# The state-space operators of an encoder layer: arithmetic in finer pieces, rotation tables staged in two smaller buffers, copies moved to ScalarE

## The chip, the cores and the metric

The kernel runs on one core of a Trainium2 chip. The metric is the device time of one launch in microseconds (us). "The profile" is one execution recorded by the hardware profiler; its times count from the first instruction (the span's start).

## What is computed

One layer of a bidirectional encoder, 512 tokens of width 1024, in float32:

```python
h = h + 0.5 * swiglu(rms_norm(h, ffn1_norm), ffn1_w_gate, ffn1_w_up, ffn1_w_down)
q, k, v, x_ssm, g_attn, g_ssm = split(rms_norm(h, mix_norm) @ w_in)
y_attn = block_gqa_attention(rope(q), rope(k), v) @ w_attn_branch
y_s5 = s5_scan(x_ssm, forward) + s5_scan(x_ssm, backward) + ssm_d * x_ssm
z = gelu(y_s5); z = z * sigmoid(z @ ssm_glu_w + ssm_glu_b)
h = h + (sigmoid(g_attn) * y_attn + sigmoid(g_ssm) * (z @ w_ssm_branch)) @ w_out
h = h + 0.5 * swiglu(rms_norm(h, ffn2_norm), ffn2_w_gate, ffn2_w_up, ffn2_w_down)
h = h + sigmoid(rms_norm(h, ple_norm) @ ple_w_gate) * (p @ ple_w_proj)
```

`s5_scan` is a linear recurrence with 64 complex states in each of 32 groups of 16 channels, in both directions: with `lam_bar = exp(lam * delta)` each state follows `s[t] = lam_bar * s[t-1] + b_bar u[t]`, and the output is the real part of `c s`.

## The kernel before

**Products.** Every float32 operand of a large product is split into a high and a low part (`split`, L539 to L541: a cast on ScalarE, a subtraction on VectorE), and three matmuls of 128x512 stand for one (`mm3`, L555 to L557). Weights come in chunks of 128 x 1024 (`wchunk`): one transfer on SP's queue (L550), one cast (`w_..h`), one subtraction (`w_..l`), with four buffers each for raw, high and low.

**The FFN** (`ffn`, f0 to f21) works in two halves. A half first makes 11 columns of gate and up (`pg`, `pu`, then L680 to L683 and a split into `ah`, `al`), then 8 output tiles `pd` that contract over those 11 columns.

**The operators of the scan.** The recurrence runs over 64 chunks of 8 tokens. The matrices for it depend on parameters alone; the generator `ssm_params` makes them beside the first FFN and spills them to DRAM, and `ssm_prefetch` brings them back for two groups at a time, in 16 blocks. Its steps: exponentials, sine and cosine, powers of `lam_bar` and their arranged copies `pa`, `pb` (L225 to L228); transposes, and their spreading into `a_d` and `b_d` by 32 transfers on POOL's queue (L249, L250); four times a table `T` of rotations for 8 groups (L269 to L271, doubling its length six times), from which ScalarE copies two `tst` tiles (L301 to L303) and VectorE adds the decay (L305, with zeros at the edges, L306, L307), each written to `d_tb` (L308); then 8 times the output matrices and the block-diagonal `bd` (L337, L340); then lags; then 8 times the input matrices, read back from `a_d` and `b_d` (L405, L406). `T` and `tst` have one buffer each.

**What sets the order.** After every piece of the FFN `side` is called with that piece's weight (`SIDE`: 5.5 for a column pair, 4.5 and 3 for an output tile of the first and second half) and writes out pieces of the generator until their weights, the numbers that it yields, have used up the credit:

```python
credit[0] += w
while credit[0] > 0:
    credit[0] -= next(gen, 1e9)
```

The framework's planner then orders each engine's instructions: an instruction may go as soon as the planner's own reckoning has its inputs and its buffer free, and what was written out earlier goes first. The order of an engine is fixed afterwards, so an instruction that really waits holds all those behind it. The same holds for SP's and POOL's queues.

Of the kernel before, what the change touches and what calls it, by code (L numbers as in the profile page):

```python
# [7 lines left out]
F32 = mybir.dt.float32  # L8
# [9 lines left out]
P = 128  # L18
SEQ = 512
G = 32  # L20
NS = 64
# [5 lines left out]
TW = 3 * GB * NC_ + 3 * GB * NC_  # L27


def split3(nc, pool, src, dst, tag, nm, rb=1):  # L30
    """src (fp32) as an exact sum of three bfloat16 parts dst[0..2], all of src's shape."""
    r = pool.tile([P] + list(src.shape[1:]), F32, tag=tag, bufs=rb, name=nm)
    nc.scalar.copy(dst[0], src)
    nc.vector.tensor_sub(r, src, dst[0])
    nc.scalar.copy(dst[1], r)
    nc.vector.tensor_sub(dst[2], r, dst[1])


def mm6(nc, o, a, b, start, stop):
    """a^T b from the parts of a and b."""  # L40
    pairs = ((0, 2), (0, 1), (0, 0), (1, 1), (1, 0), (2, 0))
    for n, (i, j) in enumerate(pairs):
        nc.tensor.matmul(o, a[i], b[j], start=start and n == 0, stop=stop and n == 5)  # L43


def ssm_params(tc, nc, pk_, px, dp, k):
    """Generator: chunked-scan operators from the SSM parameters, spilled to DRAM."""
# [61 lines left out]
    def expm1_parts(x, shape, nm, lo, hi):  # L109
        """n and e^r - 1 with x = n ln2 + r."""  # L110
        xc = sm(shape, nm + "xc")
        V.tensor_scalar(xc, x, lo, hi, ALU.max, ALU.min)
        n = sm(shape, nm + "n")
        V.tensor_scalar(n, xc, 1.4426950408889634, MAGIC, mul, add)
        V.tensor_scalar_add(n, n, -MAGIC)
        r = sm(shape, nm + "r")
        V.scalar_tensor_tensor(r, n, -0.693359375, xc, mul, add)
        V.scalar_tensor_tensor(r, n, 2.12194440e-4, r, mul, add)
        q = sm(shape, nm + "q")
        V.tensor_scalar_mul(q, r, 1.0 / 5040)  # L120
        for c in (1.0 / 720, 1.0 / 120, 1.0 / 24, 1.0 / 6, 0.5, 1.0):
            V.scalar_tensor_tensor(q, q, c, r, add, mul)
        return n, q
# [18 lines left out]
    # sin and cos of theta and of 8 theta  # L142
# [25 lines left out]
    # sin = 2 s c ; cos - 1 = -2 s^2  # L168
# [6 lines left out]
    # powers a^0 .. a^8, rows j  # L175
# [20 lines left out]
    # (lam_bar - 1) / lam  # L196
# [18 lines left out]
    # input matrix, also placed block-diagonally over the directions  # L215
# [4 lines left out]
    # powers as the operators use them: pa[r] = a^(7-r) | a^r, pb[l] = a^(l+1) | a^(8-l)  # L220
    pa, pb = sm([P, 2, G, L], "pa", pool=pk_), sm([P, 2, G, L], "pb", pool=pk_)
    for ri, src in ((0, pwr), (1, pwi)):
        sg = src.rearrange("p j g -> p g j")
        for r in range(L):
            V.tensor_copy(pa[:NS, ri, :, r], sg[:NS, :, 7 - r])  # L225
            V.tensor_copy(pa[NS:, ri, :, r], sg[NS:, :, r])
            V.tensor_copy(pb[:NS, ri, :, r], sg[:NS, :, r + 1])
            V.tensor_copy(pb[NS:, ri, :, r], sg[NS:, :, 8 - r])  # L228
    yield 9
    # chunk input operators, built with (l, channel) on the partitions  # L230
# [23 lines left out]
    # per-chunk decay and the unit rotations by 8 theta, padded with a zero at both ends  # L254
# [11 lines left out]
    def cmul2(orr, oi, a, br, bi, t):  # L266
        """As cmul, a with real and imaginary parts along its first free axis; t[i] = a b_i."""
        for i, b in ((0, br), (1, bi)):
            V.tensor_mul(t[:, i], a, b.unsqueeze(1).broadcast_to([P, 2] + list(b.shape[1:])))  # L269
        V.tensor_sub(orr, t[:, 0, 0], t[:, 1, 1])  # L270
        V.tensor_add(oi, t[:, 0, 1], t[:, 1, 0])  # L271

    GH = 8
    for gh in range(0, G, GH):
# [9 lines left out]
        while n < NC_:  # L284
            br = rkl[:, 0].unsqueeze(2).broadcast_to([P, GH, n])
            bi = rkl[:, 1].unsqueeze(2).broadcast_to([P, GH, n])
            cmul2(T[:, 0, :, 1 + n:1 + 2 * n], T[:, 1, :, 1 + n:1 + 2 * n], T[:, :, :, 1:1 + n], br, bi,
                  tb[:, :, :, :GH * n].rearrange("p a r (g n) -> p a r g n", g=GH))
            n *= 2
            if n < NC_:  # L290
                sq = pw.tile([P, 2, GH], F32, tag="sq", bufs=2, name=f"sq{gh}_{n}")
                ta = pw.tile([P, 2, 2, GH], F32, tag="sqt", name=f"sqt{gh}_{n}")
                cmul2(sq[:, 0], sq[:, 1], rkl, rkl[:, 0], rkl[:, 1], ta)
                rkl = sq
        for b in range(gh // GB, (gh + GH) // GB):
            st = pw.tile([P, TW], F32, tag="w3", name=f"tst{b}")
            g0 = b * GB - gh
            N = GB * NC_
            v = lambda i, w=1: st[:, i * N:(i + w) * N].rearrange("p (g c) -> p g c", c=NC_)
            for ri in range(2):  # L300
                nc.scalar.copy(v(ri), T[:, ri, g0:g0 + GB, 1:NC_ + 1])  # L301
                nc.scalar.copy(v(2 + ri)[:NS], T[:NS, ri, g0:g0 + GB, 0:NC_])
                nc.scalar.copy(v(2 + ri)[NS:], T[NS:, ri, g0:g0 + GB, 2:NC_ + 2])  # L303
                dv = v(4 + ri)
                V.tensor_copy(dv, e8[:, b * GB:(b + 1) * GB].unsqueeze(2).broadcast_to([P, GB, NC_]))  # L305
                V.memset(dv[:NS, :, 0], 0.0)  # L306
                V.memset(dv[NS:, :, NC_ - 1], 0.0)  # L307
            nc.sync.dma_start(d["tb"][b], st)  # L308
        yield 9
    es.close()  # L310
    pw = es.enter_context(tc.tile_pool(name="pw2", bufs=1, reuse_waits="tile"))
    # matrices, GB groups at a time: chunk output and the lags inside a chunk
    dcol = sm([P, G // 8], "dcol", pool=pk_)
    nc.gpsimd.dma_start(dcol, k["ssm_d"].rearrange("(m q) -> q m", q=P))
    kt = sm([P, 2, G, CH], "kt", pool=pk_)
    sh = [P, GB, L, CH]
    flat = lambda t: t.rearrange("p g l c -> p g (l c)")
    for b in range(NB):
# [17 lines left out]
        bd = pw.tile([P, 2, GB, 2, CH], F32, tag="bd", name=f"bd{b}")  # L336
        V.memset(bd, 0.0)  # L337
        for dr in range(2):
            ps = slice(dr * NS, (dr + 1) * NS)
            V.tensor_copy(bd[ps, :, :, dr], bb[ps, :, gs])  # L340
# [13 lines left out]
        yield 7.2  # L354
    # lag 0: both directions and D; then all lags to DRAM, lag l_out - l_in = e - 7 in column block e
# [68 lines left out]
def ssm_prefetch(nc, sp, k, j):  # L424
    """The operators of GM groups, back from DRAM."""
# [5 lines left out]
    nc.sync.dma_start(tb, d["tb"][b].rearrange("p (i n) -> p i n", i=6)[:, :, q * NC_:(q + GM) * NC_])  # L431
# [7 lines left out]
def ssm_block(nc, sp, px, pre, U, j):  # L439
    """GM groups: chunk inputs, scan over chunks, outputs in PSUM."""  # L440
# [19 lines left out]
    # states, rotated into the real axis; forward on the lower partitions, backward on the upper,  # L460
    # each written so that column n holds what enters chunk n
# [35 lines left out]
# gates before the SSM and beside it  # L497
NG1, NG2 = 8, 4
# weights of a piece of the SSM operators' arithmetic beside a piece of the FFN
# [4 lines left out]
def kernel(  # L504
# [38 lines left out]
    def wchunk(src, k, n):  # L543
        """src [(k 128), n] in DRAM -> hi, lo tiles [128, k, n]."""
# [23 lines left out]
    def rsqrt_newton(pool, ms, shape, nm, eng=V):  # L568
        """ms ** -0.5: a first guess from the bits of ms (within 4%), then Newton's steps."""
# [26 lines left out]
    class Stat:  # L596
        """Sum of squares over the features, collected tile by tile."""
# [118 lines left out]
    with tc.tile_pool(name="f1", bufs=1, reuse_waits="tile") as fp, tc.tile_pool(name="pw", bufs=1, reuse_waits="tile") as pw:  # L716
# [8 lines left out]
        def side(w):  # L725
            """Emit as much of the operators' arithmetic as fits beside a piece of the FFN."""
            credit[0] += w
            while credit[0] > 0:
                credit[0] -= next(gen, 1e9)
# [27 lines left out]
    def proj_T(c0, done):  # L757
        """In four pieces: done(u w_in[:, c0:c0 + 128] transposed)."""
# [8 lines left out]
    def run(*gens):  # L767
        """Emit pieces of the generators in turns."""
# [4 lines left out]
    def proj_tok(banks, c0, n, kn):  # L773
        """Tokens on partitions: banks[t][:, :n] = u @ w_in[:, c0:c0+n], kn contraction tiles a chunk."""
# [30 lines left out]
    with tc.tile_pool(name="qp", bufs=1, reuse_waits="tile") as qp:  # L805
# [28 lines left out]
        # channels of the SSM  # L834
# [13 lines left out]
        # q, k, v with tokens on partitions  # L848
# [23 lines left out]
        # transposed q: hi and lo parts of a head stacked on the contraction axis  # L872
# [19 lines left out]
    # the SSM runs beside the gates  # L892
# [6 lines left out]
    def scores(hd):  # L899
        """Exponentials of a head's scores, queries on partitions, and the reciprocals of their sums."""  # L900
# [44 lines left out]
    # attention: scores of a head beside the product with v of the one before  # L945
# [30 lines left out]
    # SSM gate and branch, cut into pieces that run beside the attention  # L976
# [15 lines left out]
    def half(ww, mc, x, done):  # L992
        """Two output tiles of a product with 512 contraction rows, in four pieces."""
# [140 lines left out]
def _consts():  # L1134
    """Identity, and the RoPE tables in the kernel's token order: shapes alone."""
# [37 lines left out]
```

## Time and profile before

| | us |
|---|---|
| median of 3 runs | 1213.11 |
| lowest and highest | 1210.88, 1213.55 |
| span of the profiled execution | 1211.5 |
| TensorE busy in it | 1142.5 |
| VectorE busy in it | 789.2 |
| ScalarE busy in it | 483.4 |

The profile gives the span of its execution, from the first to the last instruction, and no other time of it; beside it stand the runs' times. Engines are named PE (TensorE), DVE (VectorE), ACT (ScalarE), POOL (GpSimd) and SP (its queue issues most transfers). An engine that is idle before an instruction is shown with the length of that wait and with what ended it.

### The profile page before, as it was taken

The page shows a single profiled execution, that of the slowest core. Times are in us where ns is not written, and L with a number is a line of the kernel's source. Part 1 is how long each engine was busy: PE and PEld are TensorE (multiplying, and loading weights), DVE is VectorE, ACT ScalarE, POOL GpSimd, SP SyncE. Part 2 cuts the span into 40 slices and gives each one's busy share as a digit, 9 for nine tenths or more (in the row PEclk, how much of TensorE's full clock was granted, in tenths as well). Part 3 has the DMA queues.
Part 4 walks back from the last instruction along what each step waited for, and adds up shares of the span by engine and source line. Part 5 has one row for each costly group of instructions (what it writes and reads, how often), then busy time and mean ns, then how long its engine had stood idle before and what let it go on. Part 6 is the DMA issues. An engine that isn't in the chain of part 4 may idle for free.

```text
span 1211.5 us, 16350 instructions
## 1 busy us (share of the span) xinstructions
PE 1142.5 (94%) x6092; PEld 939.8 (78%) x6092; DVE 789.2 (65%) x1673; ACT 483.4 (40%) x834; POOL 48.7 (4%) x81
## 2 busy tenths in 40 slices
PE   4999689999999999997997999999999999999998
PEld 3787567888878877876876878888888888888886
DVE  3894588997758985998856857654443334444543
ACT  4433345453434544634365833433222223323332
POOL 4105100000000000000000000000000000000100
PEclk9999798999999999999998999999999999999999
DMA  9429746644596899787633134423223433323422
GB/s 188 129 76 271 235 138 209 196 154 139 118 263 216 273 300 174 217 252 239 207 80 95 44 79 139 122 88 104 85 71 96 133 104 88 94 72 96 142 68 52
DMA packets 258240, 177.02 MB, mean 146 GB/s; under 512 B 38672, under 2 KB 239568, under 8 KB 258160
## 3 DMA queue, kind: packets, MB, share of 16 engines
q1 hardware_dynamic: 253776, 163.70, 46.9%
q0 software_dynamic: 3920, 11.15, 3.5%
q10 hardware_dynamic: 464, 1.11, 0.5%
q8 instruction: 48, 0.79, 0.3%
q14 instruction: 32, 0.26, 0.1%
HBM read 148.89 MB, written 38.63 MB: 155 GB/s over the span
## 4 chain that ended last, share of the span: by engine, by line
PE 62%; DVE 16%; DMA 14%; issue 3%; ACT 3%; SPq 1%; POOL 0%; DVEq 0%; ACTq 0%; POOLq 0%
PE pg L555 6%; PE pg L556 6%; PE pg L557 6%; PE pd L555 5%; PE pd L557 5%; PE pd L556 5%; PE pu L555 5%; PE pu L557 5%; PE pu L556 5%; DMA d_tb<-tst 4%; DMA br<-d_b 3%; DMA w<-in_ffn_w_up_dram 2%; PE po L555 1%; PE pge L557 1%; PE po L556 1%
## 5 line engine op out<-in xcount | busy, mean ns | idle before, releaser
L682 DVE TENSOR_TENSOR t<-pu,rb 128x512 f32<-128x512 f32 x44 | 30.3, 688 | 79.0 <-PE pu L557 78.7
L680 DVE TENSOR_TENSOR t<-pg,rb 128x512 f32<-128x512 f32 x44 | 30.3, 688 | 53.4 <-PE pg L557 51.5
L540 ACT CAST ah<-t 128x512 fp32r<-128x512 f32 x44 | 27.4, 622 | 58.4 <-DVE t L683 58.3
L700 DVE SCALAR_TENSOR_TENSOR h<-pd,h 128x512 f32<-128x512 f32 x32 | 22.0, 687 | 28.7 <-PE pd L557 28.7
L681 ACT ACTIVATE t<-t 128x512 f32<-128x512 f32 x44 | 27.7, 631 | 18.2 <-DVE t L680 14.5
L541 DVE TENSOR_TENSOR al<-t,ah 128x512 fp32r<-128x512 f32 x44 | 30.2, 686 | 7.0 <-ACT ah L540 6.8
L565 ACT ACTIVATE xh<-h,gains 128x512 fp32r<-128x512 f32 x32 | 22.7, 721 | 24.6 <-DVE h L700 21.9
L683 DVE TENSOR_TENSOR t<-t,t 128x512 f32<-128x512 f32 x44 | 30.3, 688 | 2.3
L912 DVE TENSOR_REDUCE nb<-sc 128x1 f32<-128x512 f32 x32 | 21.5, 683 | 8.6 <-PE sc L911 8.3
L915 ACT ACTIVATE p<-sc,nb,rq 128x512 f32<-128x512 f32 x32 | 24.9, 782 | 4.0 <-DVE nb L913 3.8
L1078 POOL DMA_DIRECT2D pin<-in_p_dram x8 | 4.2, 532 | 546.6 <-PE pd L556 541.5
L301 ACT COPY tst<-T 128x256 f32<-128x256 f32 x16 | 6.5, 406 | 47.2 <-DVE T L270 21.6
L566 DVE SCALAR_TENSOR_TENSOR xl<-h,gains,xh 128x512 fp32r<-128x512 f32 x32 | 23.8, 744 | 0.6 <-ACT xh L565 0.3
L541 DVE TENSOR_TENSOR pl<-ppt,ph 128x512 fp32r<-128x512 f32 x32 | 21.6, 682 | 2.7 <-ACT ph L540 2.6
L305 DVE COPY tst<-e 128x256 f32<-128x256 f32 x16 | 4.0, 290 | 29.6 <-DMA d_tb<-tst 29.6
L955 PE MATMUL ppt<-ident,p 128*128 128x128 f32 x128 | 21.0, 277 | 1.1 <-ACT p L915 1.1
L642 PE MATMUL xT<-ident,xt 128*128 128x128 f32 x32 | 7.8, 424 | 14.5 <-DMA xt<-in_x_dram 14.5
L955 PEld LDWEIGHTS ppt<-ident,p 128*128 128x128 f32 x128 | 16.6, 143 | 5.7 <-ACT p L915 1.5
L540 ACT CAST ph<-ppt 128x512 fp32r<-128x512 f32 x32 | 18.4, 586 | 6.0 <-PE ppt L955 5.3
L910 PE MATMUL sc<-kh,qT 128*128 128x512 f32 x32 | 14.1, 439 | 7.0 <-ACT p L915 7.0
L43 PE MATMUL pv<-U,wv 128*128 128x64 bf16 x384 | 15.0, 199 | 4.9 <-DMA wv<-d_wv 2.8
L43 PEld LDWEIGHTS <-wv 128*128 128x128 bf16 x384 | 13.2, 101 | 7.8 <-issue 4.2
(1966 smaller groups left out, 3888.6 us busy)
## 6 DMA issues: line engine op xcount, KB each, us to landing
w<-in_ffn_w_gate_dram SPq DMA_DIRECT2D x44, 512.0 KB
w<-in_ffn_w_up_dram SPq DMA_DIRECT2D x44, 512.0 KB
w<-in_w_in_dram SPq DMA_DIRECT2D x26, 512.0 KB
w<-in_ffn_w_down_dram SPq DMA_DIRECT2D x32, 384.0 KB
w<-in_ffn_w_down_dram SPq DMA_DIRECT2D x32, 320.0 KB
d_tb<-tst SPq DMA_DIRECT2D x8, 768.0 KB
d_wo<-wo SPq DMA_DIRECT2D x8, 768.0 KB
d_wv<-wv SPq DMA_DIRECT2D x8, 768.0 KB
```

The source lines that it names most:

```text
L43: nc.tensor.matmul(o, a[i], b[j], start=start and n == 0, stop=stop and n == 5)
L540: S.copy(hi, src)
L541: V.tensor_sub(lo, src, hi.bitcast(F32))
L555: T.matmul(o, ah, bh, start=start, stop=False)
L556: T.matmul(o, ah, bl, start=False, stop=False)
L557: T.matmul(o, al, bh, start=False, stop=stop)
L680: V.tensor_mul(t1, gu[0], rb)
L681: S.activation(t1, t1, AF.Silu)
L682: V.tensor_mul(t2, gu[1], rb)
L683: V.tensor_mul(t1, t1, t2)
L915: S.activation(p_, sc, AF.Exp, bias=nb[:, t:t + 1], scale=rq[:, t, hd:hd + 1], accum_out=sm[:, t:t + 1])
L955: T.transpose(pt[:, t * P:(t + 1) * P], pr[t][:, kt * P:(kt + 1) * P], ident)
```

## The change

The powers' arranged copies and the copies into `bd` go from VectorE to ScalarE. The generator yields after each doubling of `T` and after each `tst`, and twice per output matrix, with other weights. `tst` has two buffers and holds the decay once instead of twice, so its width falls from 6 to 5 blocks of 256; `ssm_prefetch` reads the decay block twice, in a transfer of its own. Two tiles `bds` are cleared once and used in turn instead of a `bd` cleared 8 times. Comments are dropped.

```diff
-TW = 3 * GB * NC_ + 3 * GB * NC_
+TW = 5 * GB * NC_
...
         for r in range(L):
-            V.tensor_copy(pa[:NS, ri, :, r], sg[:NS, :, 7 - r])
-            V.tensor_copy(pa[NS:, ri, :, r], sg[NS:, :, r])
-            V.tensor_copy(pb[:NS, ri, :, r], sg[:NS, :, r + 1])
-            V.tensor_copy(pb[NS:, ri, :, r], sg[NS:, :, 8 - r])
-    yield 9
+            nc.scalar.copy(pa[:NS, ri, :, r], sg[:NS, :, 7 - r])
+            nc.scalar.copy(pa[NS:, ri, :, r], sg[NS:, :, r])
+            nc.scalar.copy(pb[:NS, ri, :, r], sg[:NS, :, r + 1])
+            nc.scalar.copy(pb[NS:, ri, :, r], sg[NS:, :, 8 - r])
+    yield 5
...
                 rkl = sq
+            yield 1.0 + n / 20
         for b in range(gh // GB, (gh + GH) // GB):
-            st = pw.tile([P, TW], F32, tag="w3", name=f"tst{b}")
+            st = pw.tile([P, TW], F32, tag="w3", bufs=2, name=f"tst{b}")
...
-                dv = v(4 + ri)
-                V.tensor_copy(dv, e8[:, b * GB:(b + 1) * GB].unsqueeze(2).broadcast_to([P, GB, NC_]))
-                V.memset(dv[:NS, :, 0], 0.0)
-                V.memset(dv[NS:, :, NC_ - 1], 0.0)
+            dv = v(4)
+            V.tensor_copy(dv, e8[:, b * GB:(b + 1) * GB].unsqueeze(2).broadcast_to([P, GB, NC_]))
+            V.memset(dv[:NS, :, 0], 0.0)
+            V.memset(dv[NS:, :, NC_ - 1], 0.0)
             nc.sync.dma_start(d["tb"][b], st)
-        yield 9
+            yield 0.5
...
+    bds = [pw.tile([P, 2, GB, 2, CH], F32, name=f"bd{i}") for i in range(2)]
+    for bd in bds:
+        V.memset(bd, 0.0)
...
-        bd = pw.tile([P, 2, GB, 2, CH], F32, tag="bd", name=f"bd{b}")
-        V.memset(bd, 0.0)
+        yield 4.8
+        bd = bds[b % 2]
         for dr in range(2):
             ps = slice(dr * NS, (dr + 1) * NS)
-            V.tensor_copy(bd[ps, :, :, dr], bb[ps, :, gs])
+            nc.scalar.copy(bd[ps, :, :, dr], bb[ps, :, gs])
...
-        yield 7.2
+        yield 1.6
...
-    nc.sync.dma_start(tb, d["tb"][b].rearrange("p (i n) -> p i n", i=6)[:, :, q * NC_:(q + GM) * NC_])
+    src = d["tb"][b].rearrange("p (i n) -> p i n", i=5)
+    nc.sync.dma_start(tb[:, :5], src[:, :, q * NC_:(q + GM) * NC_])
+    nc.sync.dma_start(tb[:, 5], src[:, 4, q * NC_:(q + GM) * NC_])
```

## Rows read from the trace of the kernel before

**Rows 1.** The page, part 1: busy time, share, instructions.

```profile
PE 1142.5 (94%) x6092; PEld 939.8 (78%) x6092; DVE 789.2 (65%) x1673; ACT 483.4 (40%) x834; POOL 48.7 (4%) x81
```

**Rows 2.** Stretches of 30 us: length, busy per engine, clock, DMA share, GB/s.

```profile
60.00:90.00 30.00, 29.34 (x136) 24.05 (x136) 29.29 (x118) 8.81 (x13) 1.30 (x2) 1.00 0.26 76
...
120.00:150.00 30.00, 20.42 (x76) 15.76 (x76) 15.96 (x68) 8.41 (x19) 4.69 (x8) 0.78 0.73 235
...
240.00:270.00 30.00, 30.00 (x174) 24.69 (x173) 29.46 (x56) 14.94 (x24) 0.00 (x0) 1.00 0.51 168
```

**Rows 3.** The chain that ended last, in order of time: start, us, what.

```profile
98.75 17.41 DMA d_tb<-tst
...
144.25 3.19 DMA d_tb<-tst
```

**Rows 4.** Timeline of PE, its stalls: start, us, in brackets the wait and releaser.

```profile
118.47 0.50 PE L557 MATMUL pu<-xh,w_105l 128*128 128x512 f32 x1 [2.95 <-DVE w_105l L541]
...
140.31 0.77 PE L555 MATMUL pu<-xh,w_113h 128*128 128x512 f32 x1 [9.48 <-DVE tst L307]
...
184.69 0.80 PE L555 MATMUL pd<-ah,w_137h 128*128 128x512 f32 x1 [7.85 <-ACT ah L540]
```

**Rows 5.** Timeline of DVE, 95 to 150 us: the two longest waits of L305.

```profile
116.18 0.50 DVE L305 COPY tst<-e 128x256 f32<-128x256 f32 x2 [14.52 <-DMA d_tb<-tst]
...
137.44 0.49 DVE L305 COPY tst<-e 128x256 f32<-128x256 f32 x2 [11.69 <-DMA d_tb<-tst]
```

**Rows 6.** Timelines of ACT and DVE, 181 to 185 us, ahead of the first `pd`.

```profile
181.10 0.40 ACT L301 COPY tst<-T 128x256 f32<-128x256 f32 x1 [3.08 <-DVE T L270]
...
184.03 0.62 ACT L540 CAST ah<-t 128x512 fp32r<-128x512 f32 x1
...
182.07 0.69 DVE L683 TENSOR_TENSOR t<-t,t 128x512 f32<-128x512 f32 x1
```

**Rows 7.** Timeline of POOL, 80 to 160 us: issues of the spreading transfers.

```profile
90.34 5.04 POOL L250 DMA_DIRECT2D d_a<-d_at  x8
...
107.02 0.63 POOL L249 DMA_DIRECT2D d_b<-d_bt  x1 [1.02 <-DMA d_a<-d_at]
...
129.08 0.63 POOL L249 DMA_DIRECT2D d_b<-d_bt  x1 [1.01 <-DMA d_a<-d_at]
```

**Rows 8.** Stretches of 5 us, columns as in rows 2.

```profile
120.00:125.00 5.00, 5.00 (x17) 3.87 (x17) 4.97 (x29) 1.66 (x3) 2.89 (x6) 0.69 1.02 280
...
140.00:145.00 5.00, 4.59 (x13) 3.25 (x14) 3.75 (x13) 2.98 (x8) 0.00 (x0) 0.64 0.38 108
...
155.00:160.00 5.00, 5.00 (x24) 4.14 (x23) 4.85 (x24) 1.34 (x2) 0.00 (x0) 1.00 0.26 79
...
185.00:190.00 5.00, 5.00 (x17) 3.96 (x17) 2.71 (x9) 2.10 (x6) 0.00 (x0) 0.70 1.02 283
```

**Rows 9.** Single lines: count, duration in ns (least/median/most), first and last start.

```profile
L225 DVE COPY pa<-pwr x8: 181/188/194, 1.4 to 79.7; 64x32 f32<-64x32 f32 x8
...
L337 DVE MEMSET bd<- x8: 272/272/272, 193.3 to 280.1; 128x256 f32 x8
...
L340 DVE COPY bd<-bb x16: 204/219/225, 194.9 to 282.0; 64x128 f32<-64x128 f32 x16
...
L823 ACT ACTIVATE hsq<-qs x32: 238/242/286, 493.4 to 513.8; 128x64 f32<-128x64 f32 x32
```

**Rows 10.** The prefetch: issues on SP's queue, its waits, TensorE's longest wait.

```profile
L431 SPq DMA_DIRECT2D tbl<-d_tb x16: 517/518/1278, 444.7 to 590.1; - x16
...
SPq L431 <- DVE te L471: 34.3, 13, 5.1
...
570.21 0.47 PE L43 MATMUL py<-U,ml 128*128 128x64 bf16 x6 [3.53 <-DMA ml<-d_m]
```

**Rows 11.** Timelines of ACT and PE: one weight chunk, cast and first used.

```profile
89.69 1.04 ACT L540 CAST w_97h<-w 128x1024 fp32r<-128x1024 f32 x1
...
104.02 0.39 PE L555 MATMUL pu<-xh,w_97h 128*128 128x512 f32 x1
```

## The prediction, made before the change was run

> **What bounds the kernel now.** The page's first part comes first: TensorE is busy for 1142.5 us of the 1211.5 us span [rows 1], so whatever the change brings must come out of at most 69 us in which TensorE stands, plus what a lowered clock costs it. Where that lies is read from the table of 30 us stretches [rows 2]: 60 to 90 us and 240 to 270 us are nearly full, while 120 to 150 us holds 20.42 us of matmul at a granted clock of 0.78. That is the first FFN, where the operators' arithmetic runs beside it. The chain that ended last names the reason: in order of time, the transfer `d_tb<-tst` stands in it at 98.75 with 17.41 us, and later the same transfer takes 3.19 us [rows 3].
>
> Three stalls of TensorE carry the argument [rows 4]: 2.95 us before 118.47, 9.48 us before 140.31, 7.85 us before 184.69, together 20.28 us. The first two are VectorE's. It stands 14.52 and 11.69 us at L305, the decay copy that opens the next `tst`, until the transfer of the `tst` before has landed [rows 5]. The pool holds one `tst`, L305 needs only `e8`, and the planner put it as early as its own reckoning allowed; behind it in VectorE's order stand the weights' low parts (w_105l in the first), for which TensorE waits. The third is queueing: ScalarE waits 3.08 us for table T3, copies its real and imaginary parts into `tst`, and only then casts the last `ah` of the half [rows 6], without which the first `pd` can't end.
>
> Why two transfers are slow: POOL issues the spreading of `a_d` and `b_d` in two batches, from 90.34 to about 107 and on to 129.08 [rows 7], and the 16 DMA engines are full meanwhile (share 1.02 at 120 to 125 us [rows 8]). The contended transfers land at 116.16 and 137.42, where L305 can start, 8 to 9 us after the last issue of each batch.
>
> The clock adds to each stall: 24 matmul records in 5 us are normal (155 to 160 us, clock 1.00), but 120 to 125, 140 to 145 and 185 to 190 us hold 17, 13 and 17 at clocks of 0.69, 0.64 and 0.70 [rows 8]. At 5 / 24 = 208 ns each, 7 missing are 1.5 us; in 140 to 145 us the 4.59 busy us would hold 22, so 9 are missing, 1.9 us. All three: 4.9 us. The most that the change can win here is 20.28 + 4.9 = 25.2 us.
>
> **The change part by part.**
>
> *Copies of the powers to ScalarE.* 64 copies of 64x32 leave VectorE, about 0.19 us each [rows 9]: 12.2 us off an engine that is busy 29.29 of 30 us at 60 to 90 us. TensorE is nearly full there, so this wins nothing at once; I estimate that it lets T0, the `pa` transposes and POOL's batches all start some 9 us earlier. ScalarE takes them at a price that the trace doesn't show for this shape: at least VectorE's 0.19 us (12.2 us), at most the 242 ns of its own 128x64 activation [rows 9] (15.5 us). I take the latter, nearest in form; ScalarE is busy 8.81 of 30 us at 60 to 90 us, so 15.5 us fit, and I cost it at nothing. Behind a copy that waits for the powers stand weight casts and the Silu; if that cover fails, it is rival C.
>
> [...]
>
> *Block matrices.* 8 clears of 0.272 us become 2, and 16 copies of 0.219 us go to ScalarE [rows 9]: 1.6 + 3.5 = 5.1 us off VectorE between 190 and 300 us. TensorE is full there (30.00 of 30.00 at 240 to 270 us [rows 2]), so I take zero; if ScalarE casts late instead, 16 x 0.242 = 3.9 us bounds the loss.
>
> *Two `tst`, a sixth smaller.* 768 KB become 640, so 17.41 us become 14.5 if time goes with bytes. T0's two halves now go out together and table T1 can start at once, since T too has one buffer and was held by the second half (L305 at 116.18). But the next wait is not gone: L305 of the third `tst` needs the first's slot. It needs no table, so I expect it to be hoisted into T1's work, some 3 us behind the first transfer's issue, as the row at 116.18 was. T0 and POOL's batches move together, so the transfer is again in the full stretch.
>
> First stall: 14.52 - 2.9 = 11.6 us of VectorE if nothing else changes; TensorE's 2.95 us would shrink to about nothing, or stay with the clock's 1.5 us, since two transfers now share the time. Saved between 0 and 4.5; I take 1.5, nearer the low end, because the contention is the same. Second stall, estimated from the rows moved by 9 us: the first stall ends near 106, T1 near 116, its transfer goes out near 118 and meets the rest of the second batch, which lands near 129. L305 of the fifth `tst`, near 122, then stands for 7 us instead of 11.69; TensorE saves 4.7 one for one. Bounds: 0 (as before) to 11.4 (all, with its clock). I take 6, since VectorE also has 16 us between the stalls for the weights instead of 9.5 (116.18 to 137.44 - 11.69).
>
> *Finer pieces.* The last pieces of T3 are written into the program behind f10, the last gate and up columns of the half, no longer ahead of it; with the planner's order by age the FFN's own steps come first. The floor of the third stall is two products and a cast: 0.69 + 0.69 + 0.62 = 2.0 us [rows 6]. Saved 0 to 7.85 - 2.0 + 1.5 = 7.4; I take 5, nearer the upper end. The weights of all pieces sum to 168.0 against 161.2, of 181 that the FFN offers, so the arithmetic is written out one or two output tiles later; it still ends inside the FFN, and I cost that at nothing (its cover is the 13 left over; without it the first block of the SSM waits for `wv`).
>
> *Prefetch in two transfers.* 16 more issues on SP's queue, ahead of `wo`, `m` and the weights. An issue of this line takes 0.518 us [rows 10]: between 0 (hidden, as SP stood at such an issue for VectorE anyway, 34.3 us over 13 times [rows 10]) and 16 x 0.52 = 8.3 us. TensorE does wait for `m`, 3.53 us before 570.21 [rows 10], so some is exposed: I take 1.
>
> Sum: 1.5 + 6 + 5 - 1 = 11.5 us off the profiled span of 1211.5: 1200. The runs' median, 1213.11, lies 1.6 us above that span, so 1201.6; I say 1201.5.
>
> **Rivals.**
>
> A, the forecast: the stalls shrink. 1195 to 1208. Chance 0.48.
>
> B: the second buffer takes the waits away altogether, because L305 of the third `tst` is placed behind the batch or the transfers land early. For it: outside the batches the transfer takes 3.19 us [rows 3]. Against it: in both batches it landed with the batch. 2.95 + 9.48 + 3.4 of clock + 7.4 - 1 = 22.2 off, 1190.9; say 1188 to 1195. Chance 0.25.
>
> C, slower: ScalarE becomes the bound at 50 to 90 us. Its order is fixed, and the copies wait for VectorE's chain of powers; if that is later than planned, weight casts stand behind them. The split weights have a lead: w_97 is cast at 89.69 and used at 104.02 [rows 11], 14.3 us. TensorE loses what ScalarE is late beyond it. The 15.5 us of copies in a row exceed it by 1.2; a wait as long as VectorE's longest, 14.52 us [rows 5], would make 15.7. Against A's gain of 11.5 it decides from 11.5 + 14.3 = 25.8 us on, and at 15.7 lost it gives 1217; with A's gains gone too, up to 1229. Against it: ScalarE is two thirds idle there. Chance 0.14.
>
> D: the transfers themselves bound 90 to 137 us. POOL's batches and the weights are the same, the engines are full, and a pair of `tst` lands no sooner than two in series: 2 x 14.5 us from about 90 puts the second at 119, VectorE stands for both of the next L305, and the first two gaps stay. Only the third gap's 5 us less 1 to 5 for the prefetch are won: 1209 to 1213. Chance 0.13. The Trainium skill bears on this, "DMA: Bandwidth & Descriptors", section "Queues, rings and completion order": each DMA engine takes turns between the queue rows that have work, so two `tst` on SP's row would share one turn. By that rule, with which the 17.41 us against 3.19 agrees, the time is D's.
>
> **How the numbers follow.** The predicted time is A's. A and B hold 0.73 and most of D comes on top, so the range goes from B's low end, 1188, to D's high end, 1213: about eight in ten. About 0.2%, 2.4 us, is what a measurement of this kernel can tell from no change. Faster (under 1210.7): A, B and a fifth of D, 0.76; same (to 1215.5): the rest of D, 0.10; slower: C, 0.14.
>
> **What would show it.** In the profile after: an idle time of about 10 us before one of the first four L305 and less at the next; `d_tb<-tst` still above 10 us in the chain, at 90 to 110 us; 25 or more us of matmul in 120 to 150 us; a stall of about 2 us before the first `pd`; L225 to L228 on ScalarE at about 0.24 us, and no cast long behind them. I am wrong if L305 waits nowhere (B), if TensorE shows gaps before 95 us behind casts (C), if the gaps of 3 and 9 us stand where they were (D), or if the planner's new order opens a gap behind 210 us, where nothing of this change should weigh.

## The result, and the profile after

The changed kernel takes 1198.12 us (median; 1193.93 to 1200.59) against 1213.33 us before: a ratio of 0.9864, 95% interval 0.9842 to 0.9887. The forecast was 1201.5 us, range 1188 to 1213; the time and the sign hold. Of the terms, only the sum does.

Stretches of 30 us of the profile after, columns as in [rows 2]:

```profile
90.00:120.00 30.00, 30.00 (x134) 24.86 (x133) 19.19 (x90) 10.34 (x20) 11.98 (x19) 1.00 0.97 309
120.00:150.00 30.00, 28.71 (x126) 23.14 (x126) 21.45 (x77) 13.31 (x27) 4.48 (x8) 1.00 0.73 239
150.00:180.00 30.00, 21.59 (x101) 16.68 (x100) 27.82 (x48) 18.20 (x38) 0.00 (x0) 0.83 0.58 204
```

The hole of 120 to 150 us in [rows 2] is gone, and one stands at 150 to 180 us. Timeline of TensorE, all waits of over 0.5 us between 30 and 300 us, answering to [rows 4]:

```profile
142.09 0.47 PE L561 MATMUL pg<-xh,w_127h 128*128 128x512 f32 x1 [0.58 <-DVE t L686]
...
143.50 0.50 PE L563 MATMUL pg<-xh,w_127l 128*128 128x512 f32 x1 [0.71 <-DVE w_127l L547]
...
163.70 0.50 PE L563 MATMUL pd<-ah,w_139l 128*128 128x512 f32 x1 [2.07 <-DVE w_139l L547]
...
171.34 1.44 PE L353 MATMUL pk<-bd,wo 128*128 128x96 bf16 x24 [4.60 <-ACT wo L33]
...
175.12 0.80 PE L562 MATMUL pd<-al,w_137h 128*128 128x512 f32 x1 [1.74 <-DVE al L547]
```

The stalls of 2.95 and 9.48 us have become 1.29 us in two; the third, 7.85 us, has become 8.41 us in three. VectorE still waits at the decay copy (now L306), answering to [rows 5]:

```profile
98.41 0.29 DVE L306 COPY tst<-e 128x256 f32<-128x256 f32 x1 [6.47 <-DMA d_tb<-tst]
...
117.64 0.29 DVE L306 COPY tst<-e 128x256 f32<-128x256 f32 x1 [2.50 <-DMA d_tb<-tst]
...
139.82 0.30 DVE L306 COPY tst<-e 128x256 f32<-128x256 f32 x1 [5.97 <-DMA d_tb<-tst]
```

The transfers behind those waits stand in the chain in order of time, answering to [rows 3]:

```profile
85.87 12.52 DMA d_tb<-tst
...
108.90 8.71 DMA d_tb<-tst
...
130.79 9.00 DMA d_tb<-tst
```

They still take 2.7 to 3.9 times the 3.19 us of an undisturbed one, though they are a sixth smaller. But no wait is over 6.47 us, and the split weights are far enough ahead to cover all but 1.29 us of that. Where the 12.7 us of the span came from is told by the row `pm`, the sums of squares that close the first FFN (first start) and the second (last start). Before, then after:

```profile
L614 PE MATMUL pm<-ones,ss x24: 164/250/250, 441.3 to 1154.7; 128*128 128x1 f32 x24
```

```profile
L620 PE MATMUL pm<-ones,ss x24: 164/250/251, 424.4 to 1142.0; 128*128 128x1 f32 x24
```

The first FFN ends 16.9 us earlier; from there to the end of the second FFN it takes 717.6 us against 713.4, so 4.2 us are given back in the mixers.

### The profile page after: what moved, and what is told of

Same layout as the page of the kernel before. It is cut to its first block, busy times and chain, and to the rows that moved or that the text cites. A ratio compares the mean times of both kernels' runs of the same rounds, so it can differ in the third digit from the quotient of the medians.

```text
span 1198.8 us, 16348 instructions
## 1 busy us (share of the span) xinstructions
PE 1142.1 (95%) x6092; PEld 939.0 (78%) x6092; DVE 772.8 (64%) x1563; ACT 501.7 (42%) x914; POOL 48.3 (4%) x81
## 4 chain that ended last, share of the span: by engine, by line
PE 68%; DVE 14%; DMA 9%; ACT 4%; issue 3%; SPq 3%; ACTq 0%; DVEq 0%
PE pd L562 6%; PE pd L563 6%; PE pd L561 6%; PE pg L562 6%; PE pg L563 6%; PE pg L561 6%; PE pu L563 5%; PE pu L561 5%; PE pu L562 5%; DMA d_tb<-tst 3%; DMA w<-in_ffn_w_up_dram 2%; PE pi L561 1%; PE pi L562 1%; PE pi L563 1%; SPq L403 1%
## 5 line engine op out<-in xcount | busy, mean ns | idle before, releaser
L546 ACT CAST ph<-ppt 128x512 fp32r<-128x512 f32 x32 | 18.7, 588 | 14.3 <-PE ppt L961 14.2
L43 PE MATMUL pv<-U,wv 128*128 128x64 bf16 x384 | 14.3, 195 | 9.4 <-DMA wv<-d_wv 5.7
L43 PE MATMUL py<-E,wol 128*128 128x64 bf16 x384 | 17.5, 193 | 3.2 <-DVE E L36 3.2
L33 ACT CAST E<-vv 128x256 bf16<-128x256 f32 x16 | 6.5, 404 | 29.3 <-DVE vv L479 29.1
L648 PEld LDWEIGHTS xT<-ident,xt 128*128 128x128 f32 x32 | 6.3, 223 | 15.8 <-issue 14.3
```

The source lines that it names most:

```text
L546: S.copy(hi, src)
```

## The experiments

All ratios are against the kernel before, with 95% intervals. The kernel before was timed again with each set, with medians of 1214.64 us for e1 to e4, 1216.04 for e5 to e8 and 1215.76 for e9 to e11. "Middle" is the time from the first to the last start of `pm`; the figures of 717.8 and 713.6 us in one expectation are the same distance, read at the weight loads of that row.

| | time, us | ratio | first FFN ends | middle |
|---|---|---|---|---|
| before | 1213.33 | 1 | 441.3 | 713.4 |
| changed | 1198.12 | 0.9864 (0.9842 to 0.9887) | 424.4 | 717.6 |
| e1 storage alone | 1199.02 | 0.987 (0.9829 to 0.9912) | 425.6 | 715.2 |
| e2 one `tst` | 1202.44 | 0.9907 (0.9879 to 0.9934) | 431.7 | 715.9 |
| e3 powers on VectorE | 1207.19 | 0.9945 (0.992 to 0.9971) | 429.6 | 719.3 |
| e4 coarse pieces | 1198.34 | 0.987 (0.9837 to 0.9903) | 424.6 | 715.1 |
| e5 one prefetch | 1201.75 | 0.9883 (0.9858 to 0.9908) | 424.0 | 722.7 |
| e6 `pk` by age | 1198.98 | 0.9856 (0.984 to 0.9873) | 424.0 | 716.9 |
| e7 before, spreading later | 1228.43 | 1.0095 (1.0074 to 1.0117) | 431.7 | 738.4 |
| e8 changed, spreading later | 1185.09 | 0.9752 (0.9728 to 0.9775) | 412.9 | 713.8 |
| e9 as e8, one `tst` | 1205.96 | 0.9913 (0.9881 to 0.9946) | 413.5 | 733.9 |
| e10 as e8, powers on VectorE | 1213.59 | 0.9983 (0.9959 to 1.0007) | 424.1 | 727.8 |
| e11 as e8, coarse pieces | 1187.52 | 0.9769 (0.9727 to 0.9811) | 412.1 | 715.9 |

The theory: the first two stalls came from the single `tst`, whose transfer is slowed by POOL's batches. The rivals: the finer pieces, or the copies on ScalarE, made the gain.

**e1, the storage alone.** The kernel before with `TW = 5 * GB * NC_`, `bufs=2`, one decay block and the two prefetch transfers.

> The kernel before with the storage part alone: two tst of five blocks, decay stored once, prefetch in two transfers; copies and pieces as before. Theory (the two tst take away most of VectorE's wait at the decay copy, which is what TensorE's first two stalls came from): the waits there fall from 29.6 us to about 15, the stalls of 2.95 and 9.48 us shrink to under 2 together, the third before the first pd stays near 8, the time is 1213 - 12 = about 1201. Rival (the gain needs the finer pieces or the copies on ScalarE): 1208 to 1214, with a stall of 5 us or more left between 100 and 145 us.

0.987: the whole gain. The waits fell from 29.6 to 14.5 us (two, the longest 12.7 us); TensorE stalled for 2.03 + 0.91 us at 117 us in place of 2.95 and 9.48, a little over the 2 expected, and for 2.22 + 2.16 us at the half's end, about half of the 8 expected. The first of these on TensorE's timeline:

```profile
116.92 0.47 PE L557 MATMUL pu<-xh,w_105h 128*128 128x512 f32 x1 [2.03 <-DVE t L684]
```

So the first stall stayed, as the forecast had it for the changed kernel, and the second went altogether. The two kernels reach the same time by different stalls: the changed one has no first stall, and 8.41 us at the half's end.

**e2, one buffer.**

```diff
-            st = pw.tile([P, TW], F32, tag="w3", bufs=2, name=f"tst{b}")
+            st = pw.tile([P, TW], F32, tag="w3", bufs=1, name=f"tst{b}")
```

> The changed kernel with one tst of five blocks instead of two. Theory (second buffer): the decay copy waits for over 25 us again, TensorE stalls 8 to 12 us between 90 and 145 us, and the time goes back to 1207 to 1212. Rival (the order by finer pieces and the lighter VectorE cover the wait): within 3 us of the changed kernel, 1196 to 1201.

In between: 1202.44 us. The stall is back, on TensorE's timeline of e2:

```profile
136.65 0.80 PE L563 MATMUL pu<-xh,w_113l 128*128 128x512 f32 x1 [8.10 <-DVE w_113l L547]
```

and the decay copy waits 26.6 us in all, as the theory has it; but the first of the two stalls is only 0.8 us (0.46 + 0.34), with one `tst`. The rest of the change, the narrower tile among it, is worth something by itself. By the medians that is less than the storage; the intervals of e1 and e2 overlap.

**e3, the powers on VectorE again** (the four `nc.scalar.copy` into `pa`, `pb` are `V.tensor_copy`).

> The changed kernel with the 64 copies of the powers back on VectorE. Theory (they are hidden on either engine, and only shift the operators' work by some 9 us): within 3 us of the changed kernel, 1196 to 1201, T0 finished 8 to 10 us later. Rival (the copies on ScalarE are part of the gain): 1203 to 1207, with a stall of TensorE before 100 us or a longer one at 165 to 175 us.

The theory falls: 0.9945. TensorE stalls 3.61 + 0.91 us at 119 to 121 us, the decay copy waits 14.3 us in one piece, and the first FFN ends 5.2 us later than in the changed kernel. The first stall is back:

```profile
119.41 0.47 PE L561 MATMUL pu<-xh,w_105h 128*128 128x512 f32 x1 [3.61 <-DVE t L688]
```

With e1 and e2 this says what takes it away. While the copies run on VectorE it is there with one `tst` (2.95 us, before) and with two (2.94 in e1, 4.52 here); with the copies on ScalarE it is 0.8 us with one (e2) and nothing with two. So it goes with the copies, and the second stall with the buffer. Yet e1 has the same copies on VectorE and the whole gain, so e3's loss is no price of the copies alone. The two differ in the pieces and in `bd`, which no run parts here; 1.7 us of the middle, and more between executions, aren't explained either.

**e4, coarse pieces** (`yield 9`, 9 four times, 7.2 eight times; the new yields gone).

> The changed kernel with the generator's pieces and weights as before (9, 9 four times, 7.2 eight times). Theory from the two profiles (the finer pieces did not shorten the stall of the half's end, 7.85 us before against 8.4 us in three parts after): within 3 us of the changed kernel, 1195 to 1201. Rival (the forecast's term: the finer pieces win 5 us or more there): 1203 or more, with a stall at the first pd of over 12 us, or new stalls before 150 us.

0.987: with the copies on ScalarE the finer pieces are worth nothing. Even the three stalls at the half's end are the same to 0.02 us (2.09, 4.62 and 1.73 at 163.69, 171.33 and 175.12).

**e5, one prefetch transfer.** The decay block is written to DRAM twice instead of read twice:

```diff
-            nc.sync.dma_start(d["tb"][b], st)
+            nc.sync.dma_start(d["tb"][b][:, :TW], st)
+            nc.sync.dma_start(d["tb"][b][:, TW:], st[:, 4 * N:])
```

> The changed kernel with the decay written to DRAM twice from one tst, so that the prefetch is one transfer again; all else as changed. The changed kernel needs 717.8 us from the end of the first FFN to its last gate product against 713.6 before. Theory (the split prefetch costs that): 3 to 4 us faster than the changed kernel, 1193 to 1196, with that part at 714 to 715 us. Rival (it is the planner's new order, not the split): within 2 us, with that part at 716 to 719.

The theory falls, and the rival's figure too: the middle became 722.7 us. Dropping the split doesn't win the 4.2 us back, but its own price stays unmeasured: the edit adds 8 issues on SP's queue in the FFN, and the order behind it is another. TensorE's longest stall of the middle is now 9.21 us at 645 us in the attention (behind ScalarE's `ph`), where the changed kernel has 3.55 us; what moves it is probably the planner's new order, which these runs don't take apart.

**e6, `pk` by age** (`with hp():` taken off the `pk` products).

> The changed kernel with the pk products issued by age and not ahead of the queue. Theory (the 4.6 us at 171 us are TensorE standing in order at a pk that waits for ScalarE's cast, with the last product of the half behind it): the three stalls of 8.4 us shrink to 4 or less, 1192 to 1195. Rival (VectorE and ScalarE are late with ah at the half's end whatever stands ahead on TensorE): the stall is named after ah or al and stays at 7 to 9 us, 1196 to 1201.

Half: the 4.60 us behind `pk` and the 1.74 behind `al` are gone, and 3.09 us behind `ah` stand in their place; the 2.08 us behind w_139l stayed. That is 5.2 us for 8.4, and the time is the same within its interval. Both causes act at the half's end: a product issued ahead of its age, and an `ah` that is late in any case.

**e7 and e8, the spreading held back,** in the kernel before and in the changed one. The block that makes `a_d` and `b_d` stands behind the tables, and ScalarE may take its copies only after the last copy into `tst`:

```diff
+        with tc.issue_after(lastc.ins):
+            nc.scalar.copy(sa.rearrange("p m n -> p (m n)"), pt[:, :2 * P])
...
+        with tc.issue_after(lastc.ins):
+            nc.scalar.copy(sb.rearrange("p m n -> p (m n)"), pt)
```

> The kernel before, with the spreading of a_d and b_d held back until the last table is copied, so that POOL's batches no longer run beside d_tb<-tst; one tst as before. Theory (the batches make the transfer slow): each d_tb<-tst lands in 3 to 5 us, the decay copy waits under 8 us in all, the two stalls of 2.95 and 9.48 us shrink to under 2 together and the time is 1198 to 1204. Rival (the transfer is slow beside the weights alone, or one tst is the limit): waits over 15 us, 1208 or more.

> The changed kernel with the spreading held back in the same way. Theory (what the decay copy still waits, 14.9 us, is contention that no longer stalls TensorE): the waits fall under 3 us, the time stays within 3 us of the changed kernel, 1195 to 1201. Rival (those waits still make VectorE late at the half's end): the stalls at 163 to 175 us shrink and the time is 1190 to 1194.

The contention is shown by e7. Its transfers, in the chain in order of time:

```profile
100.09 5.61 DMA d_tb<-tst
...
149.33 4.17 DMA d_tb<-tst
```

At about 100 us the same 768 KB land in 5.61 us where they took 17.41 [rows 3], the decay copy waits 8.7 us in all, and with one `tst` TensorE is full from 60 to 150 us. But the time rises by 1%. VectorE's last product of the input matrices (`wv`) starts at 457.9 us, 26 us behind the end of the first FFN (442.9 us before), and among those products stands the norm that the mixers need, so that TensorE waits for `dg`, the norm's diagonal:

```profile
456.02 2.07 PE L593 MATMUL pb<-dg,ones 128*128 128x512 f32 x2 [13.21 <-DVE dg L591]
```

The spreading now stands between the tables and the output matrices (its batches begin at 173.55 us), and VectorE has no step of the operators from 167.5 to 197.5 us.

In e8 the tables are done earlier (first batch 141.26 us). A stretch of e8:

```profile
150.00:180.00 30.00, 30.00 (x134) 24.84 (x133) 20.22 (x32) 9.72 (x17) 13.70 (x23) 1.00 0.92 276
```

TensorE is full from 30 to 320 us, no decay copy waits for a transfer, and the first FFN ends at 412.9 us: 1185.1 us, the best kernel of this study and below the rival's range. The theory falls. The rival's cause, waits that no longer stalled TensorE on the spot but made VectorE late at the half's end, isn't shown by it, for e8 changes the order too. VectorE's timeline at the half's end, first of the changed kernel, then of e8 (`m1o` opens the output matrices, this `al` is the last of the half):

```profile
154.81 0.63 DVE L329 TENSOR_TENSOR m1o<-pb,cT 128x512 f32<-128x512 f32 x1
...
174.38 0.68 DVE L547 TENSOR_TENSOR al<-t,ah 128x512 fp32r<-128x512 f32 x1
```

```profile
155.73 0.69 DVE L549 TENSOR_TENSOR al<-t,ah 128x512 fp32r<-128x512 f32 x1 [0.69 <-ACT ah L548]
...
163.52 0.63 DVE L331 TENSOR_TENSOR m1o<-pb,cT 128x512 f32<-128x512 f32 x1
```

In the changed kernel the output matrices run between the FFN's last steps of the half for 20 us. In e8 VectorE has nothing of the operators from 135 to 163 us, where the spreading stands, and the FFN has it alone. Less lateness and a later start of the output matrices come together here, and no run parts them.

**e9 to e11, parts of the change on top of e8** (edits as in e2, e3 and e4).

> The changed kernel with the spreading held back (1185.1 us) and one tst instead of two. Theory (the second buffer was needed for the contended transfers only): within 4 us of it, 1182 to 1189, the decay copy waits 5 to 20 us in pieces under 4, TensorE has no stall over 2 us before 200 us. Rival (the second buffer is worth its 4 us or more in any order): 1190 or more.

> The changed kernel with the spreading held back and the 64 copies of the powers on VectorE. Theory (the copies on ScalarE bring the operators' work forward by some 10 us, which now decides whether it ends inside the FFN): later tables by 8 to 12 us, the stage up to 200 us still without stalls, 1186 to 1195. Rival (hidden on either engine): 1182 to 1186.

> The changed kernel with the spreading held back and the pieces and weights of before. Theory (pieces decide nothing, as without the holding back): 1182 to 1189. Rival (fine pieces put the late work of the operators behind the FFN's): 1190 or more, with a stall at the half's end near 160 us or at the end of the first FFN.

e11: the theory holds, 1187.5 us; pieces decide nothing. e9: the rival, 1206 us, though the first FFN ends at 413.5 us as in e8; the loss is behind it. e10: past both ranges, 1213.6 us; its first `d_tb` goes out at 100.00 us, 14 us behind e8. Both have the sign of e7: the last `wv` product starts at 424.8 and 427.8 us, behind the first FFN's end; in e8 and e11 at 406.9 and 407.9, ahead of it. In all runs the middle is 713.8 to 722.7 us where the operators ended ahead of the first FFN (the changed kernel, e1 to e6, e8, e11) and 727.8 to 738.4 us where they ended 3.7 to 26 us behind it; the kernel before, with 1.6 us behind, has 713.4. That the lateness is the cause is shown for a part only: against e8 TensorE is busy 3.5, 7.0 and 14.4 us less in the first 30 us of the middle in e9, e10 and e7, while their middles are 20, 14 and 25 us longer. The rest lies further on in the mixers and isn't taken apart.

## Why the prediction was right, step by step

*What bounds.* Right in the main, and shown: the transfer is slow because of POOL's batches (e7), and the second stall hangs on the single `tst` (e1, e2, e3). The first hangs on the slow transfer too, but a second buffer alone doesn't take it away.

*First stall, taken as 1.5 us saved.* Mis-sized: with the clock, all 4.5 us were. For the buffer by itself the step was near: in e1 the copy waited 12.7 us where 11.6 had been forecast, and 2.94 us of stall were there. What took the stall away is the term that the forecast put at nothing, the copies of the powers (e1 to e3). In the changed kernel L306 began 6.1 us behind the transfer's issue (98.41 - 6.47 - 85.87) and not 3, and the transfer took 12.52 us instead of 14.5, so VectorE waited 6.47 us. The mechanism, a hoisted copy that waits in the batch, stood.

*Second stall, 6 us.* Mis-sized: 9.48 and its 1.9 us of clock became 1.29 us, about 10 saved. The fifth `tst`, for which 7 us were forecast, waited 2.50 us, for its slot's transfer went out at 108.90 and not near 118; the wait of 5.97 us is the seventh's, 16 us later (117.64 to 139.82 - 5.97). The price failed as well: a wait was charged to TensorE one for one, while 5.97 us cost it 1.29. The split weights were ahead by then: w_121l was made from 131.20 us and first used at 136.36.

*Third stall, 5 us by finer pieces.* This step failed. It said that age would put the FFN's steps first. The stall is 8.41 us, with 13 matmul records left at 175 to 180 us, and the pieces change nothing (e4). By the timeline the tables were done earlier, and the next work, the output matrices and their `pk`, stood at the half's end instead. The order of `pk` accounts for a part (e6). In e8 the stall is gone, with less lateness before it and no output matrices at the half's end; which of the two does it stays open.

*Copies of the powers.* Their price was right: 250 ns each, 16.0 us, where 242 ns were taken. The row after, columns as in [rows 9]:

```profile
L225 ACT COPY pa<-pwr x8: 243/250/257, 9.3 to 71.7; 64x32 f32<-64x32 f32 x8
```

The estimate that the work starts earlier was right too, 13 us for the first `tst` (85.87 for 98.75) against 9, and "costed at nothing" wrong in the good direction: the first stall went with it, and e3 and e10 lose without it. It has a price as well, since the output matrices now reach the half's end: 8.41 us of stalls there against 4.38 in e1.

*Block matrices*: zero, as TensorE is full at 180 to 300 us. *Prefetch*: 1 us was taken, and no run prices it alone; e8 has the split and a middle of 713.8 us, against 713.4 before. The 4.2 us given back in the changed kernel's middle had no other term.

Sum: about 4.5 + 10 - 1.3 + 2.6 = 15.8, near the 16.9 us of the first FFN, less 4.2. Here 1.3 is the third stall with its clock, 8.41 and an estimated 2.2 us (10 records short at 175 to 180 us) against 7.85 and 1.5, and 2.6 are small stalls of the kernel before that are gone (0.66, 0.53 and 1.40 us). The forecast's 11.5 stood beside a measured 12.7 because terms too small and one that failed cancelled. The sign rests on the mechanism; the closeness is luck. Of the rivals, C (ScalarE) and D (transfers bound) did not come. D had a pair of `tst` land no sooner than two in series, 29 us; the first landed in 12.52, and the fourth `tst` took the slot of the second without a wait at 106.14, 20 us behind the issue. B's condition did not come either, as 14.9 us of waits remain, but the first two stalls all but went, as B has it. Of the signs, the slow transfer (12.52 us) and 28.71 us of matmul at 120 to 150 us came; the wait of about 10 us and the short stall before the first `pd` did not.

## What to carry to other kernels

Ask of a second buffer how long the wait becomes and compare that with the lead of the engine behind it: the wait needn't vanish. Look for what makes the transfer slow; here moving the bulk copies (e8, 13 us more, by contention and order together) was worth nearly as much as the change itself (15 us), but only in a kernel whose side work still ended ahead of the main work. Work that runs beside a long stage has a deadline: where its steps came behind it (e7, e9, e10), the stage behind was longer, in part by a stall that can be named. And test parts in pairs: here one that the forecast put at nothing took the first stall, which the second buffer alone left standing.

## What was not expected of the hardware

An issue on SP's queue gets slower while POOL's batches run. Single line `d_tb<-tst` of the profile after, then of e8, columns as in [rows 9]:

```profile
L309 SPq DMA_DIRECT2D d_tb<-tst x8: 338/892/3371, 85.9 to 152.0; - x8
```

```profile
L286 SPq DMA_DIRECT2D d_tb<-tst x8: 332/338/339, 85.8 to 136.7; - x8
```

The same issue takes 0.34 us in e8, where no batch runs beside it, and up to 3.37 us while the DMA engines carry one. In e8 it is the weights' issues that are slow where its batches run: at most 2.30 us at 139 to 190 us, against 0.38 at 84 to 139.
